# A planner's rule for small matrix products: those on the whole array are placed at once, those on parts of it are collected, and the charges for changes of product are replaced

## The chip, the core and the metric

The kernel runs on one core of a Trainium2 chip. A core has a matrix engine (TensorE, PE in the rows; PEld is its loading of the stationary operand), a vector engine (VectorE, DVE), a scalar engine (ScalarE, ACT), GpSimd (POOL) and a queue engine (SyncE, SP), each working through its own list of instructions in order and waiting on semaphores for the others. The metric is the device time of one execution in microseconds; the kernel before is given by the median of three runs.

## The reference

Two layers of a Conformer-style block on a sequence of 512 positions with 1024 channels, everything in float32:

```python
for l in range(DEPTH):                                   # DEPTH = 2
    x = x + 0.5 * swiglu_ffn(rmsnorm(x, ffn1_norm[l]), ffn1_w_in[l], ffn1_w_out[l])
    h = rmsnorm(x, mix_norm[l])
    u_rwkv, u_gla, u_xa, u_gate = split_cols(h @ w_in[l], ...)
    y_rwkv, v_first = rwkv7_mixer(u_rwkv, v_first, ...)  # 8 heads of 64, a state of 64x64 per head
    y_gla = gla_mixer(u_gla, ...)                        # 4 heads, chunks of 64
    y_xa = memory_attention(u_xa, rmsnorm(mem, mem_norm[l]), xa_w_kv[l])
    gates = jax.nn.sigmoid(u_gate.reshape(b, s, N_BRANCH, d))
    merged = jnp.einsum('bsjc,jcd,bsjd->bsd', branches, w_branch[l], gates)
    x = x + merged @ w_out[l]
    x = x + 0.5 * swiglu_ffn(rmsnorm(x, ffn2_norm[l]), ffn2_w_in[l], ffn2_w_out[l])
return rmsnorm(x, final_norm)
```

The RWKV mixer updates its state position by position: `state = state*w + sa*(kk*a) + v*k`, and reads it with `r`.

## The kernel before

Activations lie with channels on the 128 partitions and positions along the row. **Large products** multiply a weight of 128x128 with 256 or 512 positions. To keep float32 accuracy with the array's faster input type (float32r), each operand is split into a high and a low part: ScalarE copies the high part of a weight (`whi` or `hi` from `wraw`), VectorE subtracts it for the low part (`wlo` or `lo`), and three passes are added up in PSUM (high times high, high times low, low times high). In the rows these are `ps_b<-pack,whi` and `ps_b<-pack,wlo` for the projections of the mixing stage, where a group runs whi, whi, wlo. The feed-forward layers use a scheme with seven half-size products for eight (`seven`), with their weights in `hi`, `lo`, `hl`.

**Small products** belong to the three mixers and the norms. They take plain float32 operands, and each shows as two passes (a transpose as one). Most use the whole 128x128 array: the chunk inverse of RWKV (`ps_c<-X,abd`, then `ps_c<-Z,W`, four levels), the state chain of RWKV, which for each chunk of 64 positions goes `ps_f<-qs,Z`, copies by ScalarE into `VU`, `ps_f<-VU,KBT`, an update of `S` by VectorE, `ps_y<-S,AR`, an addition into `qs` by VectorE, and again `ps_f<-qs,Z`; attention (`kT,xq`, `pt,vm`, transposes `cst,pr`), gates and sums. Others use a part of the array, 64 rows or 64 columns or both, several side by side: in RWKV `ps_i<-AR,KB` (64x128, eight per half-block), `ps_i<-VU,MA` and `ps_y<-VU,GR` (128x64, eight each per half-block), and in GLA `qe,kg`, `qr,kr`, `VT,KT` (64x64) and `qe,St` (64x128). The sequence is worked off in half-blocks of four chunks for two heads at a time, 16 over both layers.

**The order of all work comes from a planner.** The kernel's code calls engines through a `Recorder`, which only notes each operation with its dependencies (`add`) and its cost in nanoseconds (`cost`: `busy` until the engine is free, `took` until the result is there, `mode` for TensorE: whether float32r, and rows and columns of the array rounded up to 32, 64 or 128). `plan` then plays the program through in time (`run`): an operation becomes ready when all it depends on has ended, plus a hop (`lag`, 34 ns, for TensorE 214 ns from another compute engine), and each free engine takes the most urgent ready one. `plan` does this six times, each time with urgencies worked out from the order before, keeps the order whose planned end is earliest, and `issue` writes the instructions in that order. All instructions therefore carry one line of the source, L319, and are told apart by the names of what they write and read.

On TensorE the choice among ready operations is `choose`. Large products have kind 1, all others kind 0 and so come first by their key; `choose` may hold them back. When it takes a product whose mode differs from the last one's, `run` adds a charge to its planned time.

Of the kernel before, what the change touches and what calls it, by code (L numbers as in the profile page):

```python
# [287 lines left out]
class Recorder:  # L288
# [22 lines left out]
    def add(self, engine, what, a, k):  # L311
# [11 lines left out]
        for v, writes in [(v, False) for v in ins] + [(v, True) for v in outs]:  # L323
            t, area = v.tile, v.area()
            if t.free and not t.users:
                o.takes = t
            assert t.gone is None
            if not t.users or writes:
                deps.update(dict.fromkeys(t.before))
            if v.psum:  # L330

                run, old = t.runs
                if run and run[-1].engine != engine:
                    old, run = (run[-1:] if run[-1].engine == "tensor" else run), []
                deps.update(dict.fromkeys(p for p in old if p is not o))
                if run and engine == "tensor" and run[-1] is not o:
                    deps[run[-1]] = None
                t.runs = (run if run and run[-1] is o else run + [o]), old
            else:
                for p, q in t.writes:  # L340
                    if p is not o and overlap(q, area):
                        deps[p] = None
                if writes:
                    for p, q in t.reads:
                        if p is not o and overlap(q, area):
                            deps[p] = None
                (t.writes if writes else t.reads).append((o, area))
            if not t.users or t.users[-1] is not o:
                t.users.append(o)
# [66 lines left out]
        s = (400 if p.engine == "sync" else self.SLACK) if slack and o.engine == "tensor" else 0  # L416
        return self.HOP + s + (120 if o.engine == "tensor" else 0)

    HOLD = 600

    def choose(self, ready, last, est, t):

        small = [q for q in ready if q[0] == 0]
        big = min((q for q in ready if q[0]), default=None)
        if not small:
            return big
        same = [q for q in small if q[-1].mode == last]
        if same:
            return min(same)
        if big is None or (last is not None and not last[0]):  # L430
            return min(small)
        first = min(small)
        if sum(q[-1].busy for q in small) >= 400 or t - min(est[q[-1]] for q in small) >= self.HOLD:
            return first
        return big

    def run(self, late):

        import heapq
        todo = {o: len(o.deps) for o in self.ops}  # L440
        ready, free = {e: [] for e in self.ENGINES}, dict.fromkeys(self.ENGINES, 0.0)
        wait = dict.fromkeys(self.ENGINES, None)
        est = dict.fromkeys(self.ops, 0.0)
        events, count, table, last, done, dma = [], 0, None, None, 0, 0.0
        order, used, held = [], {}, {}

        def key(o):
            return (o.kind, o.n) if o.engine == "tensor" else (late[o], o.n)

        def slot(o):  # L450

            t = o.takes
            if t is None:
                return True
            k = t.pool, t.tag
            if used.get(k, 0) < t.bufs:
                used[k] = used.get(k, 0) + 1
                return True
            held.setdefault(k, []).append(o)
            return False  # L460

        def put(t, what, o):
            nonlocal count
            count += 1
            heapq.heappush(events, (t, count, what, o))

        def free_up(o):

            for q in o.next:
                g = self.lag(o, q)  # L470
                t = o.start if g is None else o.start + o.took + g
                est[q] = max(est[q], t)
                todo[q] -= 1
                if todo[q] == 0:
                    put(est[q], "ready", q)

        for o in self.ops:
            if not todo[o]:
                put(0.0, "ready", o)
        while events:  # L480
            t, _, what, o = heapq.heappop(events)
            touched = set()
            while True:
                if what == "ready":
                    if o.engine is None:
                        o.start = t
                        order.append(o)
                        free_up(o)
                        if o.tile is not None and o.tile.free:
                            k = o.tile.pool, o.tile.tag  # L490
                            used[k] -= 1
                            for q in held.pop(k, ()):
                                put(t + self.lag(o, q), "ready", q)
                    else:
                        heapq.heappush(ready[o.engine], (*key(o), o))
                        touched.add(o.engine)
                else:
                    touched.add(o)
                if events and events[0][0] <= t:
                    t, _, what, o = heapq.heappop(events)  # L500
                else:
                    break
            for e in touched:
                if free[e] > t:
                    continue
                while ready[e]:
                    if e == "tensor":
                        o = self.choose(ready[e], last, est, t)
                        ready[e].remove(o)
                        heapq.heapify(ready[e])  # L510
                        o = o[-1]
                    elif e == "scalar":
                        best = min(ready[e], key=lambda q: q[0] + (2000 if q[-1].table not in (None, table) else 0))
                        ready[e].remove(best)
                        heapq.heapify(ready[e])
                        o = best[-1]
                    else:
                        o = heapq.heappop(ready[e])[-1]
                    if slot(o):
                        break  # L520
                else:
                    continue
                o.start = t
                busy = o.busy
                if o.pipe is not None:
                    dma = max(t + 400, dma) + o.pipe
                    o.took = dma - t + o.shared + (2550 if e == "gpsimd" else 1050)
                if e == "tensor":
                    if last is not None and o.mode != last:
                        busy += 45 if o.mode[1:] == last[1:] else 92 if o.mode[1:] == (128, 128) else 190  # L530
                    last = o.mode
                if e == "scalar" and o.table is not None and o.table != table:
                    table = o.table
                    o.start += 1400
                    busy += 1400
                free[e] = t + busy
                order.append(o)
                put(free[e], "free", e)
                free_up(o)
        assert len(order) == len(self.ops), (len(order), len(self.ops))  # L540
        return order
# [1425 lines left out]
```

## Time and profile before

| | |
|---|---|
| three runs | 2490.19, 2492.41, 2492.49 us; median 2492.41 |
| profiled execution | 2490.48 us, its span 2488.6 us |
| granted TensorE clock over the span | 0.998 |
| instructions | 47065, of them 17636 matrix passes |

The profile's page gives busy time by engine, the chain of work that ended last, and groups of instructions by names and shapes. A matrix pass of TensorE is modelled with its way through the array, so passes in the timeline overlap: what a pass costs is read from start to start, not from its duration. In the timeline a row can hold several passes (x2, x10); its first number is the start of the first, its second the time to the end of the last, both in us. A shape like 128*64 is rows and columns of the array.

### The profile page before, as it was taken

The page shows a single profiled execution, that of the slowest core. Times are in us where ns is not written, and L with a number is a line of the kernel's source. Part 1 is how long each engine was busy: PE and PEld are TensorE (multiplying, and loading weights), DVE is VectorE, ACT ScalarE, POOL GpSimd, SP SyncE. Part 2 cuts the span into 40 slices and gives each one's busy share as a digit, 9 for nine tenths or more (in the row PEclk, how much of TensorE's full clock was granted, in tenths as well). Part 3 has the DMA queues.
Part 4 walks back from the last instruction along what each step waited for, and adds up shares of the span by engine and source line. Part 5 has one row for each costly group of instructions (what it writes and reads, how often), then busy time and mean ns, then how long its engine had stood idle before and what let it go on. Part 6 is the DMA issues. An engine that isn't in the chain of part 4 may idle for free.

```text
span 2488.6 us, 47065 instructions
## 1 busy us (share of the span) xinstructions
PE 2466.2 (99%) x17636; PEld 2231.3 (90%) x17636; DVE 2090.9 (84%) x4146; ACT 1452.5 (58%) x2587; POOL 241.6 (10%) x363
## 2 busy tenths in 40 slices
PE   9999999999999999999999999999999999999998
PEld 8999988888788899999989999877887888999998
DVE  8988886678888689898899889766888877898988
ACT  6665667564553456565665656674745444565655
POOL 1111100000000001211111111000000000011110
PEclk9999999999999999999999999999999999999999
DMA  6888762322222456887658787523223225568784
GB/s 198 193 202 193 176 184 77 119 72 75 78 72 79 140 166 153 210 193 187 160 132 210 192 195 180 164 87 98 84 75 85 69 75 158 147 163 212 189 191 107
DMA packets 162516, 356.97 MB, mean 143 GB/s; under 512 B 18128, under 2 KB 37008, under 8 KB 162288
## 3 DMA queue, kind: packets, MB, share of 16 engines
q1 hardware_dynamic: 124192, 287.82, 38.0%
q0 software_dynamic: 36864, 65.03, 16.5%
q8 instruction: 139, 2.28, 0.4%
q10 hardware_dynamic: 1232, 1.11, 0.1%
q14 instruction: 89, 0.73, 0.1%
HBM read 341.83 MB, written 12.06 MB: 142 GB/s over the span
## 4 chain that ended last, share of the span: by engine, by line
PE 85%; DVE 10%; issue 2%; ACT 1%; DMA 1%; SPq 0%; DVEq 0%; ACTq 0%
PE ps_b L319 42%; PE ps_i L319 24%; PE ps_f L319 9%; PE ps_c L319 8%; PE ps_y L319 1%; DVE wlo L319 1%; DVE lo L319 1%; DVE ml L319 1%; DVE s L319 1%; DVE hl L319 1%; DVE pack L319 1%; DVE x L319 1%; DVE q L319 1%; ACT whi L319 0%; DVE fm L319 0%
## 5 line engine op out<-in xcount | busy, mean ns | idle before, releaser
L319 PE MATMUL ps_b<-pack,whi 128*128 128x512 f32 (+2 forms) x2272 | 727.8, 395 | 0.6 <-DVE pack L319 0.3
L319 PEld LDWEIGHTS ps_b<-pack,whi 128*128 128x128 f32 (+1 forms) x2272 | 412.4, 187 | 82.1 <-DVE pack L319 3.2
L319 PE MATMUL ps_b<-pack,wlo 128*128 128x512 f32 (+1 forms) x1120 | 441.8, 395 | 0.6 <-DVE wlo L319 0.5
L319 DVE TENSOR_TENSOR wlo<-wraw,whi 128x1024 fp32r<-128x1024 f32 (+1 forms) x172 | 184.0, 1070 | 83.2 <-ACT whi L319 80.5
L319 PEld LDWEIGHTS ps_b<-pack,wlo 128*128 128x128 f32 x1120 | 211.1, 188 | 41.1 <-DVE wlo L319 2.9
L319 ACT ACTIVATE whi<-wraw 128x1024 fp32r<-128x1024 f32 (+1 forms) x174 | 161.9, 930 | 116.0 <-PE ps_b L319 83.4
L319 DVE TENSOR_TENSOR lo<-wraw,hi 128x1024 fp32r<-128x1024 f32 (+2 forms) x162 | 191.5, 1182 | 44.5 <-ACT hi L319 43.5
L319 ACT ACTIVATE hl<-q 128x512 fp32r<-128x512 f32 (+1 forms) x256 | 157.9, 617 | 118.0 <-PE ps_i L319 32.8
L319 ACT ACTIVATE hi<-wraw 128x1024 fp32r<-128x1024 f32 (+2 forms) x162 | 166.5, 1028 | 102.0 <-PE ps_i L319 35.6
L319 DVE TENSOR_TENSOR hl<-q,hl 128x512 fp32r<-128x512 f32 (+1 forms) x256 | 171.2, 669 | 4.7 <-ACT hl L319 3.8
L319 DVE TENSOR_TENSOR lo<-q,hi 128x1024 fp32r<-128x1024 f32 (+1 forms) x128 | 152.0, 1188 | 18.1 <-ACT hi L319 17.2
L319 ACT ACTIVATE hi<-q 128x1024 fp32r<-128x1024 f32 (+1 forms) x128 | 131.4, 1027 | 51.8 <-PE ps_b L319 45.2
L319 PE MATMUL ps_b<-pack,hi 128*128 128x256 f32 x1152 | 156.2, 277 | 0.0
L319 PEld LDWEIGHTS ps_b<-pack,hi 128*128 128x128 f32 x1152 | 143.8, 188 | 0.3
L319 PE MATMUL ps_i<-mh,hl 128*128 128x256 f32 x832 | 138.4, 278 | 0.5 <-DVE x L319 0.5
L319 PEld LDWEIGHTS ps_i<-mh,hl 128*128 128x128 f32 x832 | 119.3, 188 | 0.6 <-issue 0.6
L319 ACT ACTIVATE hl<-d 128x512 fp32r<-128x512 f32 (+1 forms) x128 | 78.9, 616 | 60.8 <-PE ps_i L319 41.4
L319 PE MATMUL ps_i<-t,hl 128*128 128x256 f32 x864 | 114.1, 281 | 0.0
L319 ACT ACTIVATE mh<-s 128x512 fp32r<-128x512 f32 (+1 forms) x156 | 90.8, 583 | 34.9 <-DVE s L319 33.5
L319 PE MATMUL ps_i<-pack,hl 128*128 128x256 f32 x864 | 110.5, 276 | 0.0
L319 PEld LDWEIGHTS ps_i<-t,hl 128*128 128x128 f32 x864 | 107.0, 189 | 0.0
L319 PEld LDWEIGHTS ps_i<-pack,hl 128*128 128x128 f32 x864 | 103.7, 188 | 0.0
(413 smaller groups left out, 6045.5 us busy)
## 6 DMA issues: line engine op xcount, KB each, us to landing
wraw<-in_w_main_dram SPq DMA_DIRECT2D x108, 512.0 KB, 3.7
wraw<-in_ffn_in_dram SPq DMA_DIRECT2D x102, 512.0 KB, 4.6
q<-in_ffn_in_dram SPq DMA_DIRECT2D x144, 256.0 KB, 4.4
d<-in_ffn_in_dram SPq DMA_DIRECT2D x72, 256.0 KB, 4.3
q<-in_ffn_in_dram POOLq DMA_DIRECT2D x72, 256.0 KB, 6.2
wraw<-in_ffn_in_dram POOLq DMA_DIRECT2D x72, 256.0 KB, 5.3
wraw<-in_ffn_out_dram SPq DMA_DIRECT2D x32, 512.0 KB, 5.9
q<-in_ffn_out_dram SPq DMA_DIRECT2D x64, 256.0 KB, 3.1
```

Source lines behind the costliest of these rows:

```text
L319: return getattr(getattr(self.tc.nc, engine), what)(*(f(v) for v in a), **{n: f(v) for n, v in k.items()})
```

## The change

Three things in the planner change, none in what is computed.

`choose`: before, every small product could be held while large ones were ready, until small products of 400 ns were collected or the oldest had been ready for 600 ns; once one was taken, all small ones that were ready followed, first those of the same mode. Now the small products on the whole array are in one queue with the large ones and go ahead of them as soon as they are ready. Only small products on a part of the array are held, until 400 ns of them are there or the oldest has been ready for 900 ns; then the most urgent is taken, and others of the same rows and columns follow it at once.

The charges: a change between large and small on the same rows and columns was 45 ns and is 0; a change to the whole array from a part was 92 and is 230; a change to a part was 190 and is 160.

The engines that an event touches are asked in a fixed order, where the order of a Python set decided before.

```diff
-    HOLD = 600
+    HOLD = 900
 
     def choose(self, ready, last, est, t):
 
-        small = [q for q in ready if q[0] == 0]
-        big = min((q for q in ready if q[0]), default=None)
-        if not small:
-            return big
-        same = [q for q in small if q[-1].mode == last]
+        full = lambda mode: mode is None or mode[1:] == (128, 128)
+        part = [q for q in ready if q[0] == 0 and not full(q[-1].mode)]
+        same = [q for q in part if q[-1].mode[1:] == last[1:]] if part and last is not None else None
         if same:
             return min(same)
-        if big is None or (last is not None and not last[0]):
-            return min(small)
-        first = min(small)
-        if sum(q[-1].busy for q in small) >= 400 or t - min(est[q[-1]] for q in small) >= self.HOLD:
-            return first
-        return big
+        whole = min((q for q in ready if q[0] or full(q[-1].mode)), default=None)
+        if not part:
+            return whole
+        if whole is None or sum(q[-1].busy for q in part) >= 400 or t - min(est[q[-1]] for q in part) >= self.HOLD:
+            return min(part)
+        return whole
...
-            for e in touched:
+            for e in self.ENGINES:
+                if e not in touched:
+                    continue
                 if free[e] > t:
                     continue
...
-                        busy += 45 if o.mode[1:] == last[1:] else 92 if o.mode[1:] == (128, 128) else 190
+                        busy += 0 if o.mode[1:] == last[1:] else 230 if o.mode[1:] == (128, 128) else 160
```

The instructions are the same in number and kind; their order on the engines changes. Two places on TensorE follow, both from the fourth half-block of RWKV in the first layer. The first is the half-block's output, eight products VU,GR on 128x64 (in the orders a product is one row, whatever its passes). Before:

```order
L319 MATMUL ps_f<-qs_6156,Z 128x128
L319 MATMUL ps_y<-VU,GR 64x64 x5
L319 MATMUL ps_b<-pack,wlo 128x512
L319 MATMUL ps_i<-wl,wzh 128x256
L319 MATMUL ps_i<-wl,wzl 128x256
L319 MATMUL ps_i<-al,wzh 128x256
L319 MATMUL ps_i<-al,wzl 128x256
L319 MATMUL ps_b<-pack,whi 128x512 x2
L319 MATMUL ps_i<-khi,blk_r 128x256 x2
L319 MATMUL ps_y<-VU,GR 64x64 x3
```

Now:

```order
L319 MATMUL ps_f<-qs_6159,Z 128x128
L319 MATMUL ps_b<-pack,whi 128x512 x2
L319 MATMUL ps_b<-pack,wlo 128x512
L319 MATMUL ps_b<-pack,whi 128x512 x2
L319 MATMUL ps_y<-VU,GR 64x64 x8
L319 MATMUL ps_b<-pack,wlo 128x512
L319 MATMUL ps_i<-AR,KB 128x128 x8
```

Before, the five products that were ready followed qs,Z at once and the last three came later; now all eight are placed together, after five large products. Over the program VU,GR stood in 31 places (15 of five, 15 of three, one of eight) and stands in 19 (13 of eight, three of five and three of three, two of these right behind VU,MA of the same shape); AR,KB stood in 19 and stands in 16, all of eight.

The second place is a link of the state chain, the third chunk of the same half-block, from qs,Z to VU,KBT. Before:

```order
L319 MATMUL ps_f<-qs_6149,Z 128x128
L319 MATMUL ps_b<-pack,wlo 128x512
L319 MATMUL ps_b<-pack,whi 128x512 x2
L319 MATMUL ps_b<-pack,wlo 128x512
L319 MATMUL ps_b<-pack,whi 128x512 x2
L319 MATMUL ps_b<-pack,wlo 128x512
L319 MATMUL ps_f<-VU,KBT 128x128
```

Now, with the link that follows:

```order
L319 MATMUL ps_f<-qs_6147,Z 128x128
L319 MATMUL ps_b<-pack,whi 128x512
L319 MATMUL ps_b<-pack,wlo 128x512
L319 MATMUL ps_b<-pack,whi 128x512 x2
L319 MATMUL ps_b<-pack,wlo 128x512
L319 MATMUL ps_f<-VU,KBT 128x128
L319 MATMUL ps_b<-pack,whi 128x512 x2
L319 MATMUL ps_b<-pack,wlo 128x512
L319 MATMUL ps_b<-pack,whi 128x512 x2
L319 MATMUL ps_y<-S_6156,AR 128x128
```

Between qs,Z and VU,KBT stood seven large products and stand five; over the program the commonest number was six (16 of 56 such links) and is four (31 of 56).

## The prediction

> **What bounds the kernel now.** I read the busy times first, then the chain that ended last, then the two stretches in which small products are mixed with large ones.
>
> ```profile
> PE 2466.2 (99%) x17636; PEld 2231.3 (90%) x17636; DVE 2090.9 (84%) x4146; ACT 1452.5 (58%) x2587; POOL 241.6 (10%) x363
> ...
> PE 85%; DVE 10%; issue 2%; ACT 1%; DMA 1%; SPq 0%; DVEq 0%; ACTq 0%
> ```
>
> The first line is busy time by engine, the second the chain by engine: TensorE has no room, and 85% of the chain is its own work. The next lines are the view by stretches, for the RWKV part of each layer (columns: length, then busy us and instructions of PE, PEld, DVE, ACT, POOL, the granted clock, DMA).
>
> ```profile
> 540.00:860.00 320.00, 317.13 (x1921) 260.38 (x1920) 258.61 (x721) 152.40 (x342) 7.26 (x29) 1.00 0.27 80
> 1750.00:2060.00 310.00, 306.75 (x1875) 251.42 (x1873) 256.80 (x706) 157.70 (x347) 5.76 (x28) 1.00 0.26 77
> ```
>
> Here VectorE is busy 258.61 of 320 us, ScalarE 152.40, the clock is 1.00. So time is won or lost on TensorE by two things alone: what it spends on changing the kind of product, and how often a product stands at its head before its operand. The change moves both.
>
> **Price of a visit to the whole array.** The rows are TensorE's timeline. In this stretch the large products run in threes (whi twice, wlo once), and small ones stand between them.
>
> ```profile
> 700.42 0.55 PE L319 MATMUL ps_c<-X,abd 128*128 128x64 f32 x4
> 700.78 0.71 PE L319 MATMUL ps_b<-pack,whi 128*128 128x512 f32 x2
> 701.33 0.40 PE L319 MATMUL ps_b<-pack,wlo 128*128 128x512 f32 x1
> 701.56 0.62 PE L319 MATMUL ps_b<-pack,whi 128*128 128x512 f32 x2
> ...
> 703.39 0.62 PE L319 MATMUL ps_b<-pack,whi 128*128 128x512 f32 x2
> 703.85 0.40 PE L319 MATMUL ps_b<-pack,wlo 128*128 128x512 f32 x1
> 704.08 0.38 PE L319 MATMUL ps_f<-qs,Z 128*128 128x128 f32 x2
> 704.22 0.71 PE L319 MATMUL ps_b<-pack,whi 128*128 128x512 f32 x2
> 704.77 0.39 PE L319 MATMUL ps_b<-pack,wlo 128*128 128x512 f32 x1
> 705.00 0.62 PE L319 MATMUL ps_b<-pack,whi 128*128 128x512 f32 x2
> ```
>
> An undisturbed three takes 704.08 - 703.39 = 0.69 us, so 0.23 per large product. With qs,Z ahead of it a three takes 705.00 - 704.08 = 0.92: the small product (two passes, x2) costs 0.23. With two small products (X,abd, four passes) it takes 701.56 - 700.42 = 1.14, so 0.45 for two. One alone costs 0.23, two together 0.45: what a visit costs beyond its products is 0.01 us, at most 0.03 with starts printed to 0.01. Collecting such products, as the planner did, gained nothing, and no longer collecting them costs 0.01 for each further visit.
>
> **Price of a visit to a part of the array.** The same view, later: three products of VU,GR on 128x64 make six passes, five make ten.
>
> ```profile
> 819.98 0.40 PE L319 MATMUL ps_b<-pack,wlo 128*128 128x512 f32 x1
> 820.22 0.38 PE L319 MATMUL ps_f<-qs,Z 128*128 128x128 f32 x2
> 820.53 0.56 PE L319 MATMUL ps_y<-VU,GR 128*64 128x64 f32 x10
> 821.02 0.73 PE L319 MATMUL ps_b<-pack,whi 128*128 128x512 f32 x2
> 821.59 0.40 PE L319 MATMUL ps_b<-pack,wlo 128*128 128x512 f32 x1
> 821.92 0.45 PE L319 MATMUL ps_y<-VU,GR 128*64 128x64 f32 x6
> 822.30 0.73 PE L319 MATMUL ps_b<-pack,whi 128*128 128x512 f32 x2
> 822.87 0.40 PE L319 MATMUL ps_b<-pack,wlo 128*128 128x512 f32 x1
> ```
>
> From wlo to wlo, less one three: 821.59 - 819.98 - 0.69 - 0.23 (qs,Z) = 0.69 for five products, and 822.87 - 821.59 - 0.69 = 0.59 for three. Two more products cost 0.10, so a product is 0.05 and the visit itself 0.59 - 0.15 = 0.44 us. The readings leave 0.38 to 0.48; I take 0.40. The Trainium skill, "TensorEngine Tiling (Array Packing)", Key Properties, says that changing the tiling mode drains TensorE; the rows agree that such a change is paid for. By the figure in "TensorE: Matmul & The Clock Gate", Single matmul latency (about 175 ns of drain), an estimate for a visit would be two drains, 0.35 us, and the sum below would come to -6.5 in place of -7.5.
>
> **The sum.** I counted stretches in the two orders; their products are the same in number and kind. Stretches of TensorE on part of the array fall from 96 to 74, mostly because VU,GR no longer comes as five and three (the first place shown with the change): 22 x 0.40 = -8.8 us. In three of the 74 one part follows another directly; half a visit each, +0.6. Stretches of small whole-array products rise from 329 to 383: 54 x 0.01 = +0.5, at most 1.6. The 128x32 large products of GLA come in 10 stretches where they came in 8; from nothing to 0.44 each, I take 0.1 each, +0.2. Together -7.5 us, bounds -10.5 (0.48, the others at nothing) to -5.3 (0.38 and 1.6, the 128x32 ones at 0.44).
>
> **What it moves towards.** A small product is now placed as soon as the plan thinks its operand is there. Waits that TensorE has today, from the view of who waited for whom on TensorE (us in total, times, longest):
>
> ```profile
> PE ps_c L319 <- DVE X L319: 1.0, 4, 0.3
> ...
> PE ps_i L319 <- DVE t L319: 0.8, 3, 0.4
> PE ps_f L319 <- ACT xq L319: 0.8, 1, 0.8
> ...
> PE ps_i L319 <- DVE KB L319: 0.6, 1, 0.6
> PE ps_b L319 <- DVE wlo L319: 0.5, 2, 0.4
> PE ps_f L319 <- DVE sg L319: 0.5, 1, 0.5
> PE ps_y L319 <- DVE S L319: 0.4, 1, 0.4
> ```
>
> The six rows of small products (all but ps_b) are 4.1 us; with the view's smaller rows of such products it is 5.0 us in 15 waits. No row of that view names a DMA, so the moved DMA issues on SP and POOL (their number stays) I cost at nothing: the weights that they bring are split by ACT and DVE before TensorE wants them, and large products waited for that split (wlo) 0.5 us in all; were that cover gone, one late weight would hold TensorE for the 1.04 us of its split (592.12 below). The tail after the last product holds the same instructions: nothing, one us either way. The fixed order in which the planner asks its engines touches no instruction: nothing.
>
> Now the links of the state chain: qs,Z, then ScalarE's two copies to VU, then VU,KBT, then VectorE's S, then S,AR, and so on, and X,abd to Z,W in the inverse. Of 232 such links, 6 had four or fewer large products and nothing else between them; in the new order 71 have. Four give 0.23 + 4 x 0.23 = 1.15 us from the first product's start to the next. What is needed, from the timeline:
>
> ```profile
> 739.47 0.46 PE L319 MATMUL ps_f<-qs,Z 128*128 128x128 f32 x2 [0.45 <-DVE sg L319]
> ...
> 739.97 0.45 ACT L319 ACTIVATE VU<-ps_f 64x64 f32<-64x64 f32 x2 [1.12 <-PE ps_f L319]
> ```
> ```profile
> 591.87 0.38 PE L319 MATMUL ps_f<-qs,Z 128*128 128x128 f32 x2
> 592.12 1.04 ACT L319 ACTIVATE whi<-wraw 128x1024 fp32r<-128x1024 f32 x1
> 593.18 0.45 ACT L319 ACTIVATE VU<-ps_f 64x64 f32<-64x64 f32 x2
> ...
> 593.94 0.38 PE L319 MATMUL ps_f<-VU,KBT 128*128 128x128 f32 x2
> ```
> ```profile
> 600.04 0.46 PE L319 MATMUL ps_f<-qs,Z 128*128 128x128 f32 x2
> 600.54 0.45 ACT L319 ACTIVATE VU<-ps_f 64x64 f32<-64x64 f32 x2 [0.20 <-PE ps_f L319]
> 601.04 0.30 PEld L319 LDWEIGHTS ps_f<-VU,KBT 128*128 128x128 f32 x2 [0.28 <-ACT VU L319]
> ```
>
> With ScalarE free the copies end 739.97 + 0.45 - 739.47 = 0.95 after qs,Z starts, and at 600.04 three large products were too few: VU,KBT started at 1.00 where 0.23 + 3 x 0.23 = 0.92 was on offer, 0.08 late. Four leave 0.15 to spare. With a split of a weight (1.04) ahead on ScalarE the operand comes at 593.63, 1.76 after, and four would be 0.6 late. Behind a late product everything on TensorE waits, the large ones too. From below, the 71 cost nothing (all like 739.47); from above, all are like 591.87: 71 x 0.6 = 43 us. I take 1.5 us, close to the lower end: the planner knows ScalarE's and VectorE's long instructions, and at 591.87 it left eight large products of room, which came out 0.31 us before need. So the forecast is -7.5 + 1.5 = -6.0.
>
> **Rivals.** *Waits take it all*: the 71 close links are each 0.1 us late, as at 600.04: +7.1, about 2492. For it: the spare 0.15 is thin. Against: 0.08 there came with three large products, not four. *Slower*: place, the same links; price, 0.6 us whenever a weight split or another 1 us instruction of ScalarE or VectorE has slipped ahead of the link's; it decides from 13 links on (13 x 0.6 = 7.8). With 25 of the 71, +15 - 7.5 = +7.5, 2499.9. For it: VectorE is busy 81% here and works in order; against: the same plan holds today's small waits at 5 us. The Trainium skill, "TensorE: Matmul & The Clock Gate", Step-by-step, says that only weight loads are pulled ahead and matmuls stay in order, which speaks for this rival; the row at 601.04, where TensorE's load stood still for ScalarE, agrees. *More than counted*: the old plan charged 45 ns for each change to and from a whole-array visit, some 560 of them, 25 us that the rows don't show (0.01 a visit). It believed TensorE later than it was; with truer charges most of the 5 us of small waits go too: -7.5 - 4 = -11.5, 2481. Against: fewer large products stand between links. That the change does not do what it says is excluded by the orders.
>
> **How the numbers follow.** The profiled execution took 2490.48 us, its span 2488.6; the median shown is 2492.41, 1.93 above that execution, and I carry this over. Span 2488.6 - 6.0 = 2482.6, execution 2484.5, median 2486.4. Chances: forecast 0.52 (its own range 2481 to 2491), waits take it all 0.22, slower 0.13, more than counted 0.13. About 0.2% (5 us) is what a measurement can tell from no change. Faster by more, below 2487.4: all of the last case and two thirds of the forecast, 0.47. Slower: 0.13 and a little of the second case, 0.15. Within: 0.38. The range 2478 to 2497 holds the forecast, the second case, most of the last and the mild part of the slower one.
>
> **What would show it.** In the new trace, the number of VU,GR rows in the timeline with x16 rises and those with x6 and x10 go; visits of six passes still cost 0.59. The row of qs,Z alone between large products still adds 0.23. TensorE's waits for ACT VU, DVE qs, S and W show whether the close links hold: under 8 us in all for the forecast, 12 for no change, 20 for slower. Wrong would be a stall that moves to the large products (waits for wlo or whi of many us), or a visit to part of the array that costs little where it no longer stands beside a small whole-array product.

## The result and the profile after

| | before | after |
|---|---|---|
| median of six runs each, in turn on one chip | 2492.03 us (2490.17 to 2493.35) | 2477.85 us (2475.78 to 2479.34) |
| ratio | | 0.9942, 95% interval 0.9931 to 0.9952 |
| profiled execution, its span | 2490.48, 2488.6 us | 2475.78, 2473.9 us |
| TensorE busy; span less busy | 2466.2; 22.4 us | 2457.0; 16.9 us |

The change gains 14.2 us; 6.0 were forecast. Of the 14.7 us between the two spans, 5.5 are time in which TensorE stood and 9.2 are busy time.

The page after, busy time by engine and the chain that ended last by engine (85% TensorE and 10% VectorE before):

```profile
PE 2457.0 (99%) x17636; PEld 2221.7 (90%) x17636; DVE 2087.5 (84%) x4146; ACT 1457.3 (59%) x2587; POOL 242.0 (10%) x363
...
PE 96%; DVE 2%; ACT 1%; issue 1%; DMA 0%; DVEq 0%; ACTq 0%
```

VectorE's share of the chain has fallen to 2%. The two RWKV stretches after, in the view by stretches:

```profile
540.00:860.00 320.00, 319.55 (x1945) 260.43 (x1944) 263.02 (x740) 158.18 (x352) 8.32 (x30) 1.00 0.28 84
1750.00:2060.00 310.00, 309.03 (x1903) 251.87 (x1902) 257.19 (x727) 161.49 (x351) 7.57 (x29) 1.00 0.28 84
```

In these 630 us TensorE stood for 2.87 + 3.25 = 6.12 us before and stands for 0.45 + 0.97 = 1.42 now, and it gets through 24 and 28 more passes in the same time.

The visits, in TensorE's timeline after:

```profile
734.08 0.50 PE L319 MATMUL ps_b<-pack,wlo 128*128 128x512 f32 x1
734.41 0.40 PE L319 MATMUL ps_b<-pack,whi 128*128 128x512 f32 x1
734.74 0.69 PE L319 MATMUL ps_y<-VU,GR 128*64 128x64 f32 x16
735.35 0.50 PE L319 MATMUL ps_b<-pack,whi 128*128 128x512 f32 x1
735.69 0.40 PE L319 MATMUL ps_b<-pack,wlo 128*128 128x512 f32 x1
735.92 0.62 PE L319 MATMUL ps_b<-pack,whi 128*128 128x512 f32 x2
```

From 734.41 to 735.92 are one visit and three large products: 1.51 - 0.69 = 0.82 us for eight VU,GR, where the forecast's readings give 0.44 + 8 x 0.05 = 0.84, and 0.80 with the 0.40 that it took. In the whole timeline VU,GR stands 13 times as x16, three times as x10 and three as x6; before it was once, 15 and 15 times.

What TensorE's weight loads waited for, in the five links of small products (us in total, times, longest). Before:

```profile
PEld ps_f L319 <- DVE qs L319: 1.6, 6, 0.5
...
PEld ps_y L319 <- DVE S L319: 1.4, 4, 0.9
...
PEld ps_c L319 <- DVE W L319: 1.4, 6, 0.3
...
PEld ps_f L319 <- ACT VU L319: 1.2, 3, 0.7
```

After:

```profile
PEld ps_f L319 <- DVE qs L319: 4.3, 14, 0.5
...
PEld ps_c L319 <- DVE X L319: 3.7, 11, 0.6
PEld ps_f L319 <- ACT VU L319: 3.3, 10, 1.1
...
PEld ps_c L319 <- DVE W L319: 3.2, 11, 0.6
...
PEld ps_y L319 <- DVE S L319: 2.5, 11, 0.3
```

The close links are there: 5.6 us of waits before, 17.0 after (before, X is not among the loads' waits). But of the five operands only VU also shows as a wait of a product (0.7 us, once): a load runs ahead of its product. The links are late by a little and cost little. What has become less is on the other side, VectorE's waits for small products. Before:

```profile
DVE S L319 <- PE ps_f L319: 17.2, 10, 3.0
...
DVE W L319 <- PE ps_c L319: 12.0, 17, 1.4
```

After:

```profile
DVE S L319 <- PE ps_f L319: 7.1, 6, 2.0
...
DVE W L319 <- PE ps_c L319: 4.5, 7, 1.0
```

With Z, qs and MA, the other operations of VectorE that wait for a small product of RWKV, it is 43.7 us before and 27.9 after. VectorE works in order, so what stands behind such a wait is late too: the operands KB, X, t, wlo and ml, for which TensorE's products waited 3.9 us before, name no wait of a product after. That the one follows from the other is a reading of two traces; the experiments below bear it out only in part. Other waits came in their place (rt 1.2 us, ps_i 1.1, hi 1.6 for 1.1), and all waits of TensorE's products that have a name fell from 11.7 to 8.9 us.

I also worked through both traces from product to product: what each kind takes undisturbed, from start to start, times its number; what the changes to a part of the array and back take; and what is left over, the waits. The last large product starts 13.5 us earlier (2463.04 for 2476.50), and what stands behind it is 1.2 us shorter. Of the 13.5, the changes are 6 to 9 (6.2 if only the ends of a visit are counted, 8.8 with the time between its products) and the waits 5 to 7. In the two RWKV stretches alone TensorE stands 4.7 us less.

### The profile page after: what moved, and what is told of

The parts are those of the page before. It is cut to its first block, busy times and chain, and to the rows that moved or that the text cites. A ratio compares the mean times of both kernels' runs of the same rounds, so it can differ in the third digit from the quotient of the medians.

```text
span 2473.9 us, 47041 instructions
## 1 busy us (share of the span) xinstructions
PE 2457.0 (99%) x17636; PEld 2221.7 (90%) x17636; DVE 2087.5 (84%) x4146; ACT 1457.3 (59%) x2587; POOL 242.0 (10%) x363
## 3 DMA queue, kind: packets, MB, share of 16 engines
q0 software_dynamic: 36864, 65.03, 16.6%
## 4 chain that ended last, share of the span: by engine, by line
PE 96%; DVE 2%; ACT 1%; issue 1%; DMA 0%; DVEq 0%; ACTq 0%
PE ps_b L319 47%; PE ps_i L319 27%; PE ps_f L319 10%; PE ps_c L319 9%; PE ps_y L319 1%; DVE pack L319 0%; DVE wlo L319 0%; DVE xn L319 0%; ACT xrh L319 0%; DVE x L319 0%; DMA yd<-sg 0%; DVE xrl L319 0%; DMA x<-in_x_dram 0%; DVE sqa L319 0%; ACT whi L319 0%
```

## The experiments

All are built from the changed or the old planner. Medians stand beside runs of the kernel before on the same chip (2490.7 to 2492.2 us). A visit is a stretch of small products between large ones; a link is the way from one small product of the RWKV chain to the next, a close one has four or fewer large products in it. For each kernel two numbers of its trace stand beside the time: the time that TensorE stands in the two RWKV stretches (630 us less the two busy times), and the waits of its loads for qs, VU, S, W and X. The change itself was timed on another chip than the rest, and the kernel before differs by up to 1.5 us between chips; a difference to the change of 2 us therefore says little.

| kernel | small whole-array products | charges ns (whole; from part, to part) | room ns | TensorE stands us | loads wait us | median us |
|---|---|---|---|---|---|---|
| before | held, 400 or 600 ns | 45; 92, 190 | 60 | 6.1 | 5.6 | 2492.0 |
| e1 charges alone | held | 0; 230, 160 | 60 | 6.5 | 2.4 | 2487.4 |
| e2 rule alone | at once | 45; 92, 190 | 60 | 4.8 | 28.3 | 2486.7 |
| **the change** | at once | 0; 230, 160 | 60 | 1.4 | 17.0 | 2477.9 |
| e8 | at once | 45; 230, 160 | 60 | 5.7 | 35.4 | 2492.3 |
| e3 | at once, parts too | 0; 230, 160 | 60 | 1.6 | 16.0 | 2481.2 |
| e4 | held, and parts as in the change | 0; 230, 160 | 60 | 9.4 | 10.8 | 2492.6 |
| e11 | held, 200 or 300 ns | 0; 230, 160 | 60 | 2.1 | 12.8 | 2476.1 |
| e9 | at once | 0; 230, 160 | 200 | 1.5 | 12.3 | 2473.9 |
| e10 | at once | 45; 230, 160 | 200 | 4.6 | 21.8 | 2485.0 |
| e12 | at once | 0; 92, 190 | 60 | 1.9 | 15.8 | 2470.5 |
| e13 | at once | 0; 30, 60 | 60 | 0.8 | 13.1 | 2469.7 |
| e14 | at once | 0; 330, 260 | 60 | 3.0 | 19.6 | 2479.1 |
| e15 | at once | 0; 92, 190 | 200 | 1.5 | 7.3 | 2469.6 |

"Room" is what the plan adds between an operand's end and the product on TensorE that reads it, beside its hops.

### The two halves of the change, and the 45 ns alone

The charges with the old rule:

```diff
-                        busy += 45 if o.mode[1:] == last[1:] else 92 if o.mode[1:] == (128, 128) else 190
+                        busy += 0 if o.mode[1:] == last[1:] else 230 if o.mode[1:] == (128, 128) else 160
```

> Only the three charges are changed; the old rule holds every small product, 600 ns as before. Stretches on a part of the array: 94 (96 before, 74 after), close links of the chain: 8 of 232 (6 and 71), so by the price of a visit alone it gains 2 x 0.40 = 0.8 us. Theory A (true charges remove TensorE's waits, about 7 us of the 14): about 2484 us. Theory B (small products placed at once remove them): about 2491 us, no change.

The new rule and HOLD 900 with the old charges (the line above as it was):

> Only the rule and its 900 ns; the old charges 45, 92, 190 stay. Stretches on a part: 73, close links 74, so by visits alone -8 us. Theory A (true charges remove the waits): the waits stay, about 2484 us. Theory B (placing at once removes them): about 2477 us, like the whole change.

Measured: 2487.41 us, ratio 0.9981 (0.9972 to 0.9990), and 2486.68, ratio 0.9979 (0.9970 to 0.9989). Each half is worth 4 to 5 us and the whole 14: together they do what neither does alone, and neither theory had given these numbers. With the charges alone, TensorE stands as long as before; with the rule alone, the loads' waits at the links are five times those of before. Then the change with only the 45 ns put back:

```diff
-                        busy += 0 if o.mode[1:] == last[1:] else 230 if o.mode[1:] == (128, 128) else 160
+                        busy += 45 if o.mode[1:] == last[1:] else 230 if o.mode[1:] == (128, 128) else 160
```

> The changed kernel with one charge put back: 45 ns for a change between large and small on the whole array; 230 and 160 for parts stay. Stretches on a part 74, close links 79. If it is this charge that leaves close links late (the plan counts 0.09 us for each visit between that the chip does not take): waits as with the rule alone under the old charges, about 2486 us. If the charges for parts matter instead: like the whole change, 2478.

Measured: 2492.29 us, ratio 1.0005 (0.9995 to 1.0014). This one number takes the whole gain away, 6 us more than was expected of it, and the links show where. The loads' waits in this kernel:

```profile
PEld ps_f L319 <- ACT VU L319: 10.8, 32, 1.2
PEld ps_f L319 <- DVE qs L319: 9.6, 25, 0.7
...
PEld ps_y L319 <- DVE S L319: 6.8, 27, 0.7
PEld ps_c L319 <- DVE W L319: 6.2, 21, 0.6
...
PEld ps_c L319 <- DVE X L319: 2.0, 6, 0.5
```

35.4 us, 18.4 more than with the change; the profiled span is 19.6 longer (the median 14.4). One such link in its timeline:

```profile
632.97 0.38 PE L319 MATMUL ps_f<-qs,Z 128*128 128x128 f32 x2
...
633.11 0.71 PE L319 MATMUL ps_b<-pack,whi 128*128 128x512 f32 x2
...
633.57 0.45 ACT L319 ACTIVATE VU<-ps_f 64x64 f32<-64x64 f32 x2
633.65 0.40 PE L319 MATMUL ps_b<-pack,wlo 128*128 128x512 f32 x1
634.07 0.30 PEld L319 LDWEIGHTS ps_f<-VU,KBT 128*128 128x128 f32 x2 [0.45 <-ACT VU L319]
634.07 0.49 PE L319 MATMUL ps_f<-VU,KBT 128*128 128x128 f32 x2
```

Three large products stand in the link, and VU,KBT starts 634.07 - 632.97 = 1.10 after qs,Z where 0.23 + 3 x 0.23 = 0.92 was on offer: 0.18 late. Charges that TensorE doesn't spend, 45 ns into a visit and 45 out of it, fill the link in the plan, so fewer large products seem enough to it. VectorE's waits don't tell the two kernels apart: for S, W, Z, qs and MA they are 27.0 us here and 27.9 in the change.

### Holding

Nothing held, parts neither:

```diff
-        if whole is None or sum(q[-1].busy for q in part) >= 400 or t - min(est[q[-1]] for q in part) >= self.HOLD:
+        if whole is None or min(part) < whole:
```

> New charges; no small product is held, those on a part neither. Stretches on a part: 94, close links 66. By the visits it is 0.8 us apart from the kernel before and 8 us above the changed one. Theory B (placing at once removes 7 us of waits): about 2486 us. If the gain is all in the visits: about 2493 us. Theory A gives 2486 us too, since the charges are true here.

Parts as in the change, but small whole-array products held again, by the old 400 ns of work or 600 ns of time:

```diff
-        whole = min((q for q in ready if q[0] or full(q[-1].mode)), default=None)
...
+        some = [q for q in ready if q[0] == 0 and full(q[-1].mode)]
...
+        if sum(q[-1].busy for q in some) >= 400 or t - min(est[q[-1]] for q in some) >= 600:
+            return min(some)
+        return big
```

> New charges; small products on a part are collected as in the change, those on the whole array are held too (400 ns, 600 ns) as before. Stretches on a part: 78, close links 15. By visits -7 us. Theory A (true charges): -7 - 7, about 2478 us. Theory B (placing at once): the waits stay, about 2485 us.

Measured: 2481.18 us, ratio 0.9959 (0.9944 to 0.9973), and 2492.58, ratio 1.0003 (0.9994 to 1.0013). Both lie outside what either theory gave, the first 5 us below, the second 8 us above. Without collecting, the parts are visited 94 times in place of 74. That is 20 x 0.40 = 8.0 us more; by the count from product to product some 8 more for changes and some 3 less for waits, 5.2 in the span (3.3 in the medians). So collecting parts is worth having, but less than its visits.

The second kernel looked like proof that a held product costs by itself. Its trace shows something narrower. TensorE's rows at one place, which comes in both layers:

```profile
636.82 0.49 PE L319 MATMUL ps_y<-S,AR 128*128 128x128 f32 x2 [0.55 <-DVE S L319]
...
638.07 0.49 PE L319 MATMUL ps_f<-qs,Z 128*128 128x128 f32 x2 [0.76 <-DVE qs L319]
...
639.47 0.80 PE L319 MATMUL ps_f<-VU,KBT 128*128 128x128 f32 x2 [0.92 <-ACT VU L319]
```

The same places in its view by stretches (busy us of PE, PEld, DVE, ACT, POOL, then the granted clock and DMA):

```profile
636.00:639.00 3.00, 1.25 (x7) 0.67 (x5) 2.22 (x6) 1.58 (x5) 0.00 (x0) 0.99 0.43 99
639.00:645.00 6.00, 5.49 (x23) 3.86 (x23) 2.94 (x11) 3.69 (x9) 0.10 (x1) 0.50 0.18 73
1874.00:1878.00 4.00, 1.49 (x7) 0.89 (x6) 3.26 (x11) 2.53 (x8) 0.10 (x1) 1.00 0.45 146
1878.00:1881.00 3.00, 2.94 (x12) 2.42 (x13) 1.90 (x8) 1.61 (x4) 0.00 (x0) 0.50 0.08 29
```

Here the state chain runs with no large product between its links. TensorE stands three times in a row, and its clock is halved: in the first layer at 638.9, within the third stand, for 6.8 us; in the second at 1878.0, behind the third, for 3.4. The halved clock costs about 5 us (half of 10.2) and the standing 0.55 + 0.76 + 0.92 = 2.2 in each layer: some 9 of the 14.7 us by which this kernel is slower than the change, in two places. The Trainium skill, "TensorE: Matmul & The Clock Gate", HAM oscillation, warns of idle gaps of over about 3.4 us. The trace differs from that, and it decides: no gap there was over 0.92 us, and the clock fell. So a run was made with half the holding:

```diff
-        if sum(q[-1].busy for q in some) >= 400 or t - min(est[q[-1]] for q in some) >= 600:
+        if sum(q[-1].busy for q in some) >= 200 or t - min(est[q[-1]] for q in some) >= 300:
```

> Small whole-array products held again beside those on parts, but for 300 ns or 200 ns of work in place of 600 and 400 (with those the time was 2492.6). Visits to parts 74, as in the change. If holding costs in proportion, by VectorE standing: about half of the 14.7 us, 2483 to 2487, VectorE's idle time on small products between 34 and 66 us. If the loss came from two places alone, where TensorE stood so long that its clock was halved: 2478 to 2481 and no halved clock.

Measured: 2476.10 us, ratio 0.9941 (0.9926 to 0.9956), below both ranges; no halved clock before the last large product (2462.0; the clock fell at 2464.0), and VectorE's waits for S and W as short as in the change:

```profile
DVE S L319 <- PE ps_f L319: 7.9, 10, 2.0
...
DVE W L319 <- PE ps_c L319: 4.3, 5, 1.3
```

My theory that holding costs in proportion has fallen: half the holding costs nothing. What the full hold brought is a chain that runs bare in two places, which is some 9 us, and longer waits of VectorE (58.2 us for S, W, Z, qs and MA, 23.1 with half the hold, 27.9 in the change). What the waits of VectorE cost by themselves is not shown.

### The price of a visit

The change with 40 products more, whose results nothing reads, put singly, one after each 40 large products; they came to stand in the first feed-forward stretch. On 128x64 of the array, then on the whole array ([:128, :64]), then on 128x64 in five groups of eight:

```diff
...
+                        if seen % 40 == 0 and seen >= 200:
+                            for _ in range(1):
+                                one = self.dum_one.make()
+                                self.tc.nc.tensor.matmul(self.dum.make()[:64, :64], one.to_broadcast([P, 64]),
+                                                         one.to_broadcast([P, 64]), start=True, stop=True)
...
```

> The changed kernel with 40 extra products on 128x64 (64 positions, two passes) put singly between large products of 256 positions in the last feed-forward layer; the order of all else stays, and their results are not used. If a visit to a part costs 0.40 us beyond the product's 0.05: +18 us, about 2496. If the visit was mis-sized and costs only half: +10, about 2488.

> The same with 40 extra products on the whole array (128x128, 64 positions, two passes): 0.23 us each with 0.01 for the visit, +9 us, about 2487. If a visit to the whole array costs the 0.09 us that the old charges took for its two changes: +13, about 2491.

> The same 40 products on 128x64, but in five visits of eight: 40 x 0.05 + 5 x 0.40, +4 us, about 2482. If the visits cost nothing and each product carries its share: as with 40 single ones.

Measured: 2498.88, 2485.27 and 2483.53 us, ratios 1.0027 (1.0014 to 1.0040), 0.9976 (0.9966 to 0.9986) and 0.9967 (0.9954 to 0.9980). Against the change that is +21.0, +7.4 and +5.7 us: 0.53 for each single product on a part, 0.19 for each on the whole array, 1.1 for a group of eight (1.3 if both are measured from the kernel before on their own chip). One of the single ones and one of the groups:

```profile
153.61 1.10 PE L319 MATMUL ps_b<-pack,hi 128*128 128x256 f32 x8
154.65 0.33 PE L595 MATMUL ps_y<-one 128*64 128x64 f32 x2
154.91 0.75 PE L319 MATMUL ps_b<-pack,lo 128*128 128x256 f32 x4
155.49 0.76 PE L319 MATMUL ps_i<-t,hl 128*128 128x256 f32 x5
```

```profile
91.48 0.28 PE L319 MATMUL ps_c<-ml,hi 128*128 128x256 f32 x1
91.69 1.14 PE L595 MATMUL ps_y<-one 128*64 128x64 f32 x16
92.77 0.38 PE L319 MATMUL ps_c<-mh,hi 128*128 128x256 f32 x1
92.99 0.28 PE L319 MATMUL ps_b<-mh,hi 128*128 128x256 f32 x1
```

Twelve large products take 1.36 us there (shown below), so the single one adds 1.88 - 1.36 = 0.52. The group adds 1.51 - 0.23 = 1.28. Seven products more are 0.76, 0.11 each (all on one part; VU,GR lie side by side, at 0.05), which leaves 0.41 for the visit. The forecast's 0.40 stands.

### Room at the links, and the charges for parts

```diff
-    HOP, SLACK = 34, 60
+    HOP, SLACK = 34, 200
```

> The change, with 200 ns in place of 60 that the plan allows between an operand's end and the product on TensorE. Close links 40 (71 in the change), visits to parts 75 (74). Theory that late links hold TensorE: its weight loads' waits for VU, qs, S, W and X (17 us in the change) fall to about 7, and the time to 2472 to 2476. Theory that held products cost by making VectorE stand: 140 ns more for each link keeps small products back a little, time 2479 to 2484. If neither counts any more: 2478.

The same edit with the 45 ns put back:

> The change with the 45 ns charge put back, which alone lost the whole gain (2492.3), and with 200 ns of room in place of 60. If the charge hurt because it left TensorE's links 0.09 us short for each visit, the room gives that back: 2478 to 2484, waits of the weight loads for VU, qs, S, W and X under 20 us (35 with the charge alone). If the charge hurts in another way (the order of all other work), 2489 or more.

Measured: 2473.93 us, ratio 0.9933 (0.9918 to 0.9948), and 2484.99, ratio 0.9976 (0.9967 to 0.9986). More room takes 3 to 4 us off the change and 7 off the kernel with the false charge, where the loads' waits fall from 35.4 to 21.8: about half of its harm was links that were too short. In the change the waits fell less than expected (12.3, not 7). VectorE's wait before S, 17.2 us in the kernel before and 7.1 in the change, is long again with more room, and the time falls all the same:

```profile
DVE S L319 <- PE ps_f L319: 16.5, 15, 2.6
```

For S, W, Z, qs and MA together it is 34.7 us there. The old charges for parts, lower ones and higher ones:

```diff
-                        busy += 0 if o.mode[1:] == last[1:] else 230 if o.mode[1:] == (128, 128) else 160
+                        busy += 0 if o.mode[1:] == last[1:] else 92 if o.mode[1:] == (128, 128) else 190
```

> The change with the old charges for visits to parts (92 and 190 ns in place of 230 and 160), that between whole-array products staying 0. Visits 73. If only the charge between whole-array products decides: 2476 to 2480. If the charges for parts matter as well, whose visits the plan then holds 0.1 us too cheap: 2482 or more.

> The change with the charges for visits to parts of the array lower still (30 and 60 ns; 230 and 160 in the change, 92 and 190 in the last run, 2470.5). Visits 77 (74), +1.3 us by themselves. If a charge that is too high makes links late, and those of 230 and 160 still are: 2468 to 2473, loads' waits for VU, qs, S, W and X under 16 us. If the last run was quicker by the accident of its order: 2476 to 2482.

> The change with the charges for visits to parts 100 ns higher each (330 and 260). Visits 67, 7 fewer, -3 us by themselves. If too high a charge makes links late, as the 45 ns between whole-array products did: 2482 to 2488, loads' waits for the five operands 22 us or more. If the charge for parts does not act on the links: 2473 to 2477.

Measured: 2470.48 us, ratio 0.9919 (0.9904 to 0.9933); 2469.68, ratio 0.9912 (0.9896 to 0.9929); 2479.06, ratio 0.9951 (0.9937 to 0.9966). I had expected no difference from the old charges; they are 7 us quicker than the ones "as traced". The rule alone (old charges, 2486.7) against the same with 230 and 160 (2492.3) says the same a second time. The two numbers of the table don't show where these 7 us come from: TensorE stands 1.9 us for 1.4 in the change, the loads wait 15.8 for 17.0. Higher charges fell between the two expectations: 1.2 us slower than the change with 7 visits fewer, which by themselves are 3 us less, and with 2.6 us more of the loads' waits. Yet 230 + 160 = 0.39 us is what a visit costs. So a charge need not be false to do harm. That a plan which counts too little for TensorE leaves every operand time to spare, as room does, fits all of these runs; no run isolates it. Room on top of the old charges:

> Charges 0, 92 and 190 with 200 ns of room at the links in place of 60. Close links 33. If late links are what is left to gain: 2464 to 2468 (the room gave 4 us in the change itself), waits of the loads for the five operands about 10 us. If the room was an accident of one order: 2470 or more.

Measured: 2469.59 us, ratio 0.9915 (0.9900 to 0.9929). The loads' waits halve again, to 7.3, and the time does not move: the products behind those loads wait 0.5 us in both kernels, the rest is hidden by loads that run ahead. The best kernels of the series are these three near 2470, 6 to 8 us faster than the change and 20 to 22 faster than before; they can't be told apart.

### Is it the order's accident?

Differences of 4 to 8 us were by now read as causes. As a test, an edit that should do nothing:

```diff
-    HOP, SLACK = 34, 60
+    HOP, SLACK = 34, 70
```

> The change with 70 ns of room in place of 60: too little to matter to a link, enough to reorder the rest. A measure of what an order's accidents are worth. If the times of the series follow their causes: 2476 to 2480. If reordering alone moves them by several us: outside that.

Measured: 2484.34 us, ratio 0.9974 (0.9964 to 0.9984): 6.5 us slower than the change. But TensorE stands 2.6 us in RWKV (1.4 in the change) and the loads wait 16.6 (17.0). The loss lies in the first feed-forward stretch, without any wait. From 120 to 280 us, in the view by stretches of this run:

```profile
120.00:280.00 160.00, 160.00 (x1366) 160.00 (x1365) 136.38 (x232) 94.57 (x161) 29.37 (x34) 1.00 0.80 192
```

And of the change:

```profile
120.00:280.00 160.00, 160.00 (x1403) 160.00 (x1403) 138.88 (x240) 97.35 (x166) 30.22 (x35) 1.00 0.80 197
```

TensorE is busy throughout and at full clock in both, but gets through 37 passes fewer. There the weights' buffer `hl` had been placed behind the buffer that `xl` and later `ml` use (from byte 221056 of each partition) in place of ahead of it (206528). Two runs keep every instruction in its order and move only these buffers, one each way:

```diff
+                for v in o.outs if first and o.engine is not None else ():
+                    if v.tile.pool.name == "ffn" and v.tile.tag == "fhl":
+                        next(t for t in v.tile.pool.tiles if t.tag == "m23l").make()
+                        first = False
+                        break
                 o.call()
```

> The change, every instruction in its order, but the buffers of the first feed-forward stretch placed as in the run with 70 ns of room: the weights' tile hl behind xl and ml (from byte 221056 of each partition) in place of ahead of them (206528). If the place of the buffers is what made that run slow: 1044 products that read hl, 6.6 ns more each, +6.9, so 2484 to 2486, and 120 ns from product to product in that stretch where the change has 113. If it was the order: 2477 to 2479.

> The run with 70 ns of room (2484.3), every instruction in its order, with hl placed ahead of xl and ml again (from byte 206528). If the place of the buffers made it slow: 2476 to 2479, as the change itself, and 113 ns from product to product in the first feed-forward stretch. If the order did: 2483 to 2486.

Measured: 2484.73 us, ratio 0.9971 (0.9961 to 0.9982), for the change with hl moved behind; 2477.96, ratio 0.9946 (0.9932 to 0.9959), for the run with 70 ns and hl ahead again. Twelve products that read hl, in the change:

```profile
151.09 1.52 PE L319 MATMUL ps_f<-pack,hl 128*128 128x256 f32 x12
152.45 1.52 PE L319 MATMUL ps_i<-pack,hl 128*128 128x256 f32 x12
```

The same with hl moved behind:

```profile
153.19 1.60 PE L319 MATMUL ps_f<-pack,hl 128*128 128x256 f32 x12
154.63 1.60 PE L319 MATMUL ps_i<-pack,hl 128*128 128x256 f32 x12
```

1.36 us against 1.44, 113 ns a product against 120. I had taken the whole loss for the 1044 products that read hl; the two traces, compared product by product, say otherwise. With hl moved the stretch is 7.6 us longer: 4.5 behind products that read hl and 2.9 behind those that read hi and lo, which lie in another pool. And the 216 products t,hl did not become slower (118 ns in both). So the place of the two buffers made that run slow; which operand is slowed by what is open. With them put back, a reordering without a cause moved the time by 0.1 us. That is one such reordering; it speaks for reading the other differences as causes, without proving it for each. In the traces of the kernels of the table, products that read hl follow each other in this stretch as in the change (115 ns in the mean, 119 with the buffers moved); in the kernel before they do so too, so the gain of the change does not come from there.

## Why the prediction was right or wrong

- *Price of a visit to a part* (0.40 taken, 0.38 to 0.48): right. 0.41 by the group of eight, 0.53 for a single product with its visit, 0.82 in the new trace for eight VU,GR.
- *Price of a visit to the whole array* (0.01): right as far as it can be seen. In the new trace a single product between large ones still adds 0.24 us in the median; the added ones cost 0.19 where 0.23 was expected.
- *The sum* (-7.5, bounds -10.5 to -5.3): right. Worked from product to product the changes went down by 6 to 9 us.
- *What it moves towards* (+1.5): this step failed, in its sign. Waits went down by 5 to 7 us, 4.7 of them as standing of TensorE in the two RWKV stretches. I counted what the new links would add and took the waits of today as a floor that only grows. The close links did get late, 57 times for 17.0 us at the loads, but the products behind them waited 0.7 us. And the waits of today were no floor: with rule and charges changed together most of the standing in RWKV went. That the 45 ns must go for this is shown, since they bring it back (5.7 us of standing). Why the old waits went is in part open. My reading is that held products had made VectorE stand (43.7 us for five operations, 27.9 now), and that what came behind them on VectorE was late for TensorE. Against it, VectorE's waits do not order the kernels: they are 27.0 us in the slow one with the 45 ns and 34.7 in the faster one with more room.
- *The tail* (nothing, one us either way): 1.2 us less behind the last large product, from the order at the end.
- *More than counted* (chance 0.13, -11.5): the nearest of the rivals, and its reason, the false 45 ns, is the one that decided: put back, it takes the whole gain. But it expected the charge to act by itself on the 5 us of small waits. With the old rule all three charges together are worth 4 us; with the new one the 45 ns alone are worth 14. My point against it, fewer large products between links, did not hold: the links were closer and the products behind them hardly waited.
- *Waits take it all* and *slower*: neither came with the change. The kernel with the 45 ns has late links (111 waits of the loads, 35.4 us) and no gain, as in *waits take it all*; that its 2492.3 us meet the 2492 given there is luck, since the sum there was 71 links of 0.1 us. *Slower* was seen in no kernel with the same work.
- *What would show it*: x16 rose from 1 to 13, x10 and x6 went to three each, eight VU,GR cost what the prices say, and TensorE's products wait 0.7 us for VU and too little for qs, S and W to be listed, under the 8 us of the forecast. That count was the wrong gauge: it was 0.6 us before (S and VU) and shows none of what was won.
- *The fixed order in which the planner asks its engines*: nothing was forecast; it was not tried by itself.
- The range's lower end, 2478.0, lay 0.15 us above the median. It was drawn from *more than counted* with the old waits as the most that could be won.

## What to carry to other kernels

Existing waits belong in the sum as something that can go, not only as a floor to which a change adds. For that, read also the waits of the engine that feeds the bottleneck: VectorE's 17.2 us for one operation stood in the trace before, and I never read that view. How much of such a wait reaches the bottleneck has to be tried, since here it did not order the kernels. In a planned order, rule and charge must be tried together: the 45 ns that the engine doesn't pay cost 14 us with the rule that places products at once, all three old charges 4 us with the one that holds them. A little too much room (200 ns for 60) or too low a charge cost nothing here and gained 3 to 8 us. Before a few microseconds between two orders are explained, look whether the same products run at the same pitch in a stretch without waits.

## What the runs showed of the hardware

- The place of two buffers in memory set the pitch of products: twelve that read hl take 1.36 us with hl from byte 206528 of the partition and 1.44 from 221056 (113 and 120 ns each), with the same instructions in the same order, at full clock and with no wait in the trace. The Trainium skill, "SBUF — State Buffer", SBUF: two separate sides, says that TensorE's port never waits on anyone; whatever the cause, these runs show products slowed by places alone. Which access disturbs which is open: xl and ml moved together with hl, products that read hi and lo became slower too (2.9 of the 7.6 us), and t,hl did not.
- The granted clock halved after about 3 us in which TensorE was busy 1.25 us of 3.00, with no gap over 0.92 us, and stayed so for 6.8 us; in the second layer it was 1.49 us of 4.00, and 3.4 us. A small wait at a link that stands bare thus costs more than itself.
- Weight loads waited 15.8 us for the links' operands in one of the fastest kernels and 7.3 in another, with the same time (2470.5 and 2469.6): a wait of a load is not yet a wait of TensorE.
